# Raw left factors of the down projections in a queue of their own, loaded one use ahead of their split

## Chip, core and metric

The kernel runs on one core of a Trainium2 chip. The metric is the device time of one execution in microseconds (us). Before the change it is 1993.24 us, the median of three runs (1992.93 to 1993.47).

## The reference

One layer of a decoder trunk for 1024 prompt rows and 64 sample rows: an FFN (SwiGLU, 1024 to 2816 to 1024), a mixer (window attention and a gated linear recurrence side by side, between the projections `w_in` and `w_out`), and a second FFN, each between RMS norms and with a residual. All in float32. What the change concerns is the down projection of both FFNs:

```
def swiglu(x, w_gu, w_down):
    g, u = jnp.split(x @ w_gu, 2, axis=-1)
    return (jax.nn.silu(g) * u) @ w_down
```

## The kernel before

The 1088 rows stand in three blocks: block 0 (320 rows, the sample rows among them), and blocks 1 and 2 (384 rows each). A float32 product is made of three matmuls (`mm3`, L277 to L281): each operand is split into a rounded high part and a low rest. `split` (L257 to L259) does this with a cast on ScalarE (L258) and a subtraction on VectorE (L259).

Block 0's down projection is computed plainly (`down`, L906). Blocks 1 and 2 go together through a Strassen-like scheme of seven products, numbered 1 to 7. The up projection forms the left factors, seven for each pair of FFN columns, and stores them in DRAM as `FA` (L790, L792), and the right factors as `FB` and `FH`. The `pair` function (L995) reads them back: for each product m it runs over six groups of column pairs (`GROUPS`, five of two and one of one), and a group of two takes 18 matmuls, for three PSUM banks. `put` then adds a bank to the outputs on VectorE (L975), or for a product that starts an output copies it on ScalarE (L985 for product 5).

`begin_pair(ms, inner)` (L936) makes two queues for a list of products: `W`, the right factors, two ahead, and `AC`, the left factors, two ahead with inner=True and one ahead otherwise. A queue is an `Ahead` (L74): a list of functions, each of which issues a load and the split of its tile; `next` hands out the oldest tile and calls as many further functions as the depth asks for.

In a left factor's function, `act(m, ks)`, four things stand together: the tile `t` for the split halves, a raw tile (`ar` in the profile), its load from `FA` on SP's queue (L962), and the split. `t` is always one of eight slots named `h384` (`hslot(1)`, L67). The raw tile is one of four slots `wf` with inner=True; with inner=False it takes one of the same eight `h384` slots. These slots also hold `hmix[1]` and `hmix[2]`, the split inputs of `w_in` for blocks 1 and 2, four slots each (`new_h`, L302, called by `pre_n`, L444).

The first FFN runs its products as PA = (1, 6, 2) with inner=True, before the mixer; then (5, 3), (7,) and (4,) with inner=False, while the mixer of block 0 and the norms of blocks 1 and 2 run in between, in small portions at each `tick()`. The second FFN runs PA, (5, 3), (7,) and (4,), all with inner=True, at the kernel's end. The `last` argument of `down` and `pair` begins the next pair's queues before the last group of the current one.

Weights of products 1, 2, 3, 5 and 6 are loaded raw (L947, L950; three slots `raw`) and split into two of eight slots `wsp`; 7 and 4 of the first FFN are loaded as split halves (L941, L942).

SP issues nearly all loads, in order. The order of the instructions on each engine, and which slot a tile gets, are made by the kernel's scheduler from the program's order and a timeline of its own (`schedule_with_timeline_sim=True`, L1749); a tile may so be loaded long before the place where the program names it, if a slot is free.

Of the kernel before, what the change touches and what calls it, by code (L numbers as in the profile page):

```python
# [45 lines left out]
def tile_step(ctx: ExitStack, tc: tile.TileContext, A: dict, O: list):  # L46
# [10 lines left out]
    def uid(s):  # L57
        cnt[0] += 1
        return f"{s}_{cnt[0]}"
# [7 lines left out]
    def hslot(n):  # L67
        w = WIDTH[n]
        return pp.tile([P, 4, w], F32R, tag=f"h{w}", bufs=8 if w == 384 else 4, name=uid("h"))
# [20 lines left out]
    def rawslot(shape=(P, KC, P)):  # L90
        return pp.tile(list(shape), F32, tag="raw", bufs=NRAW, name=uid("raw"))
# [165 lines left out]
    def split(hi, lo, src, lo_eng=None):  # L257
        S.copy(hi, src)  # L258
        (lo_eng or V).tensor_tensor(lo, src, hi.bitcast(F32), op=ALU.subtract)  # L259
# [389 lines left out]
    def make_ffn(wgu, wdn, h, tag):  # L649
# [284 lines left out]
        GROUPS = [range(k, min(k + 2, NK)) for k in range(0, NK, 2)]  # L934

        def begin_pair(ms, inner):  # L936
            def weight(m, ks):
                n, k0 = len(ks), ks[0]
                if m in halves:
                    hi, lo = [pp.tile([P, 2, 512], F32R, tag="wsp", bufs=8, name=uid("w")) for _ in range(2)]  # L940
                    nc.sync.dma_start(hi[:, :n].bitcast(F32), FH[:, k0:k0 + n, halves[m]])  # L941
                    nc.sync.dma_start(lo[:, :n].bitcast(F32), FB[:, k0:k0 + n, {7: 0, 4: 2}[m]])  # L942
                    return hi, lo
                raw = rawslot((P, 2, 512))
                if m in (1, 2, 3):
                    r, half = (k0 if m == 1 else k0 + NK), m == 3
                    nc.sync.dma_start(raw[:, :n], wdn[r * P:(r + n) * P, half * 512:half * 512 + 512].rearrange(  # L947
                        "(k p) m -> p k m", p=P))
                else:
                    nc.sync.dma_start(raw[:, :n], FB[:, k0:k0 + n, {7: 0, 5: 1, 4: 2, 6: 3}[m]])  # L950
                hi, lo = [pp.tile([P, 2, 512], F32R, tag="wsp", bufs=8, name=uid("w")) for _ in range(2)]
                split(hi[:, :n], lo[:, :n], raw[:, :n])
                return hi, lo

            def act(m, ks):
                n, k0 = len(ks), ks[0]
                t = hslot(1).rearrange("p (k l) w -> p k l w", k=2)
                if inner:
                    raw = f.pool.tile([P, 2, 384], F32, tag="wf", bufs=4, name=uid("ar"))
                else:  # L960
                    raw = pp.tile([P, 2, 384], F32, tag="h384", bufs=8, name=uid("ar"))
                nc.sync.dma_start(raw[:, :n], FA[:, k0:k0 + n, SLOT[m]])  # L962
                split(t[:, :n, 1], t[:, :n, 0], raw[:, :n])
                return t

            W[ms] = Ahead([lambda m=m, ks=ks: weight(m, ks) for m in ms for ks in GROUPS])
            AC[ms] = Ahead([lambda m=m, ks=ks: act(m, ks) for m in ms for ks in GROUPS], 2 if inner else 1)
            W[ms].fill()
            AC[ms].fill()
# [595 lines left out]
    act, unit0, scaled = pre_first(xs[0], rows1, f1pre, h, [f1.raw0(c) for c in (first[0] * P, DFF + first[0] * P)], w0, part)  # L1565
# [187 lines left out]
```

## Time and profile before

| what | before |
|---|---|
| median of three runs | 1993.24 us |
| the profiled execution's own time | 1993.22 us |
| its span, first to last instruction | 1991.5 us |
| granted clock of TensorE, mean | 0.999 |
| loads `ar` from `FA` | 70 of 384 KB, 14 of 192 KB |
| data moved by DMA | 370.31 MB, 186 GB/s |
| FFN 1 pair PA, about | 576 to 646 us |
| FFN 1 pairs (5, 3), (7,), (4,), about | 728 to 846 us |
| FFN 2 pairs, about | 1822 to 1984 us |

A line of the profile gives an engine, the program's line (L258 is line 258), the operation, and the tiles as out<-in. PE is TensorE, PEld its weight loads, DVE VectorE, ACT ScalarE, POOL GpSimd; SPq is the queue of SP that issues loads. In a timeline the first two columns are start and duration in us, a bracket at the end is the idle time of the engine before the instruction and what ended it. In a list of waits stand the total in us, the number of times and the longest. Matmuls are pipelined, so one that is listed with 0.39 us can start 0.22 us after the one before it.

### The profile page before, as it was taken

To read this page: it belongs to the slowest core of one execution; us is meant where nothing else is said; L and a number is where in the kernel's file an instruction comes from. 1 tells how busy PE (TensorE), PEld (TensorE's weight loads), DVE (VectorE), ACT (ScalarE), POOL (GpSimd) and SP (SyncE) were. 2 spreads that over 40 slices of the span, in tenths; PEclk is the share of its full clock that TensorE was granted. 3 is DMA by queue.
4 is the path that set the end of the run, shared out by engine and by line. 5 is a ranking of instruction groups with operands and counts; after the bars stand their busy time and mean duration, and the time that the engine had idled before them with its cause. 6 is when DMAs were issued, how large, how long until landed. Compare 5 with 4: busy or idle time off the path is not lost.

```text
span 1991.5 us, 34618 instructions
## 1 busy us (share of the span) xinstructions
PE 1978.7 (99%) x13331; PEld 1854.6 (93%) x13331; DVE 1406.9 (71%) x2595; ACT 949.0 (48%) x1736; POOL 178.0 (9%) x244
## 2 busy tenths in 40 slices
PE   9999999999999999999999999999999999999998
PEld 8999999999998987797999898989999999999886
DVE  7686767886558656777667756756887877655667
ACT  5753334444445444445344444756544444444453
POOL 0000000000004101211113311220000000000201
PEclk9999999999999999999999999999999999999999
DMA  8735555755677647766434343527565555677874
GB/s 230 225 107 186 175 170 177 232 196 192 228 243 212 182 138 236 251 169 181 128 104 132 92 138 107 177 90 237 165 210 191 197 183 193 209 232 232 291 262 140
DMA packets 377319, 370.31 MB, mean 186 GB/s; under 512 B 40546, under 2 KB 294321, under 8 KB 377137
## 3 DMA queue, kind: packets, MB, share of 16 engines
q1 hardware_dynamic: 371169, 357.21, 56.9%
q10 hardware_dynamic: 5984, 10.88, 1.6%
q8 instruction: 105, 1.72, 0.4%
q14 instruction: 61, 0.50, 0.1%
HBM read 284.31 MB, written 84.71 MB: 185 GB/s over the span
## 4 chain that ended last, share of the span: by engine, by line
PE 96%; DMA 1%; DVE 1%; ACT 1%; issue 0%; SPq 0%; DVEq 0%; ACTq 0%
PE mm L279 28%; PE mm L280 28%; PE mm L281 28%; PE pv L1219 1%; PE c L281 1%; PE c L279 1%; PE c L280 1%; PE sc L1178 1%; PE pT L1206 1%; PE tr L511 1%; DMA ar<-fa 1%; PE lv L1251 1%; PE l L1274 0%; DMA raw<-in_ffn_w_gu_dram 0%; DMA xt<-in_x_prompt_dram 0%; PE av L1329 0%
## 5 line engine op out<-in xcount | busy, mean ns | idle before, releaser
L279 PE MATMUL mm<-h,wsph 128*128 128x320 f32 (+1 forms) x1280 | 407.3, 319 | 0.0
L280 PE MATMUL mm<-h,wsph 128*128 128x320 f32 (+1 forms) x1280 | 405.3, 317 | 0.0
L281 PE MATMUL mm<-h,wspl 128*128 128x320 f32 (+1 forms) x1280 | 403.6, 317 | 0.0
L258 ACT CAST wsph<-raw 128x1024 fp32r<-128x1024 f32 x200 | 209.1, 1048 | 269.6 <-PE mm L280 213.7
L259 DVE TENSOR_TENSOR wspl<-raw,wsph 128x1024 fp32r<-128x1024 f32 x200 | 247.7, 1240 | 125.3 <-ACT wsph L258 120.7
L258 ACT CAST w<-raw 128x512 fp32r<-128x512 f32 (+1 forms) x218 | 160.3, 740 | 209.2 <-PE mm L280 111.9
L259 DVE TENSOR_TENSOR w<-raw,w 128x512 fp32r<-128x512 f32 (+1 forms) x218 | 185.8, 856 | 87.6 <-ACT w L258 87.1
L279 PEld LDWEIGHTS mm<-h,wsph 128*128 128x128 f32 x1280 | 240.2, 188 | 3.8 <-issue 2.8
L281 PEld LDWEIGHTS mm<-h,wspl 128*128 128x128 f32 x1280 | 239.9, 188 | 2.8 <-issue 2.3
L280 PEld LDWEIGHTS mm<-h,wsph 128*128 128x128 f32 x1280 | 240.5, 188 | 1.5 <-issue 1.1
L279 PE MATMUL mm<-h,w 128*128 128x384 f32 (+1 forms) x720 | 240.3, 335 | 0.6 <-ACT w L258 0.5
L280 PE MATMUL mm<-h,w 128*128 128x384 f32 (+1 forms) x720 | 240.7, 335 | 0.0
L281 PE MATMUL mm<-h,w 128*128 128x384 f32 (+1 forms) x720 | 235.4, 334 | 0.0
L279 PE MATMUL mm<-w,h 128*128 128x512 f32 x462 | 181.1, 395 | 0.6 <-DVE big L975 0.6
L280 PE MATMUL mm<-w,h 128*128 128x512 f32 x462 | 181.3, 392 | 0.0
L281 PE MATMUL mm<-w,h 128*128 128x512 f32 x462 | 179.8, 391 | 0.0
L280 PE MATMUL mm<-big,w 128*128 128x384 f32 x528 | 176.5, 334 | 0.0
L279 PE MATMUL mm<-big,w 128*128 128x384 f32 x528 | 176.3, 334 | 0.0
L281 PE MATMUL mm<-big,w 128*128 128x384 f32 x528 | 176.2, 334 | 0.0
L279 PEld LDWEIGHTS mm<-h,w 128*128 128x128 f32 x720 | 135.0, 188 | 1.3 <-ACT w L258 0.7
L280 PEld LDWEIGHTS mm<-h,w 128*128 128x128 f32 x720 | 135.1, 188 | 0.1
L281 PEld LDWEIGHTS mm<-h,w 128*128 128x128 f32 x720 | 134.7, 188 | 0.1
(363 smaller groups left out, 3576.0 us busy)
## 6 DMA issues: line engine op xcount, KB each, us to landing
raw<-in_ffn_w_gu_dram SPq DMA_DIRECT2D x156, 512.0 KB
raw<-in_ffn_w_down_dram SPq DMA_DIRECT2D x74, 512.0 KB
raw<-in_w_in_dram SPq DMA_DIRECT2D x54, 512.0 KB
ar<-fa SPq DMA_DIRECT2D x70, 384.0 KB
big<-in_ffn_w_down_dram SPq DMA_DIRECT2D x88, 256.0 KB
fb<-big SPq DMA_DIRECT2D x44, 512.0 KB
fa<-big SPq DMA_DIRECT2D x22, 768.0 KB
raw<-fb SPq DMA_DIRECT2D x30, 512.0 KB
```

What stands on the lines that cost most here:

```text
L258: S.copy(hi, src)
L259: (lo_eng or V).tensor_tensor(lo, src, hi.bitcast(F32), op=ALU.subtract)
L279: PE.matmul(out, a[0], b[0], start=first, stop=False, skip_group_check=resume)
L280: PE.matmul(out, a[0], b[1], start=False, stop=False, skip_group_check=resume)
L281: return PE.matmul(out, a[1], b[0], start=False, stop=last, skip_group_check=resume).ins
L511: PE.transpose(bank[:, i * P:(i + 1) * P], y[kh][:, i, k * P:(k + 1) * P], ident)
L1178: PE.matmul(banks[g][:, i * 256:i * 256 + wk], zq[64 * g:64 * g + 64, 2 * pr + i, b * P:(b + 1) * P], kx[64 * g:64 * g + 64, k0:k0 + wk], ...
L1206: PE.transpose(bank[:, (i * nk + kb) * P:(i * nk + kb + 1) * P], pt[g][:, i, kb * P:(kb + 1) * P], ident)
L1219: PE.matmul(ob[:, hd * 64:hd * 64 + 64], pT[g][:, (i * nk + kb) * P:(i * nk + kb + 1) * P], vn[:, vb, g * 64:g * 64 + 64], start=kb == 0, ...
L1251: PE.matmul(b5[cs, n_, a], x[:, a, cs], y[:, a, cs], start=True, stop=True)
```

## The change

`act` loses its raw tile and its load to a new function `act_raw`; a second `Ahead` of depth 1, local to `begin_pair`, holds the raw tiles of all products and groups in the same order. `act` allocates `t` and then takes the next raw tile from this queue, and the queue issues the load of the following raw tile before `act` splits the one it took. The ring of slots is the same as before in either case. Loads, splits, their number and size are unchanged; `begin_pair` no longer issues as many loads as splits at its start, but one more.

```diff
-            def act(m, ks):
+            def act_raw(m, ks):
                 n, k0 = len(ks), ks[0]
-                t = hslot(1).rearrange("p (k l) w -> p k l w", k=2)
                 if inner:
                     raw = f.pool.tile([P, 2, 384], F32, tag="wf", bufs=4, name=uid("ar"))
                 else:
                     raw = pp.tile([P, 2, 384], F32, tag="h384", bufs=8, name=uid("ar"))
                 nc.sync.dma_start(raw[:, :n], FA[:, k0:k0 + n, SLOT[m]])
-                split(t[:, :n, 1], t[:, :n, 0], raw[:, :n])
+                return raw[:, :n]
+
+            raw = Ahead([lambda m=m, ks=ks: act_raw(m, ks) for m in ms for ks in GROUPS], 1)
+
+            def act(m, ks):
+                n = len(ks)
+                t = hslot(1).rearrange("p (k l) w -> p k l w", k=2)
+                split(t[:, :n, 1], t[:, :n, 0], raw.next())
                 return t
```

## Prediction

> **What bounds the kernel now.** I read the page first: busy time by engine, then the chain that ended last.
>
> ```profile
> PE 1978.7 (99%) x13331; PEld 1854.6 (93%) x13331; DVE 1406.9 (71%) x2595; ACT 949.0 (48%) x1736; POOL 178.0 (9%) x244
> PE 96%; DMA 1%; DVE 1%; ACT 1%; issue 0%; SPq 0%; DVEq 0%; ACTq 0%
> ```
>
> TensorE is busy for 1978.7 of 1991.5 us, and 96% of the chain is TensorE's own work. The change adds and removes no matmul, so it can gain only where TensorE stands still: 12.8 us in all. The second view, the waits of TensorE alone (us in total, times, longest), says where:
>
> ```profile
> PE ax L566 <- DVE sm L570: 1.1, 1, 1.1
> PE lv L1251 <- DVE big L1369: 1.1, 1, 1.1
> PE tr L598 <- DMA big<-in_x_sample_dram: 0.8, 1, 0.8
> PE mm L279 <- ACT wsph L258: 0.6, 1, 0.6
> PE mm L279 <- DVE big L975: 0.6, 2, 0.4
> PE mm L279 <- ACT w L258: 0.5, 1, 0.5
> PE spv L1405 <- DVE t L1400: 0.4, 1, 0.4
> ```
>
> They sum to 5.1 us; the rest is the stretch after the last matmul. Three (ax, tr and w) belong to the kernel's start, with the first rows of x. That leaves 1.1 + 0.6 + 0.6 + 0.4 = 2.7 us of waits in the whole body, whatever their cause. This is the bound on any gain by shorter waits.
>
> Third, what the tile `ar` (the raw left factor) makes others wait for, once as a row of all waits and once for 600 to 860 us alone:
>
> ```profile
> ACT h L258 <- DMA ar<-fa: 36.6, 16, 6.1
> ```
>
> ```profile
>   DMA ar<-fa: 36.6, 16
> ```
>
> ScalarE sits for 36.6 us on loads of `ar` from FA, all of it between 600 and 860 us. Those are the pairs of the first FFN called with inner=False (products 5, 3, 7, 4); the 36.6 us are the change's target. But ScalarE is 48% busy: its idle time counts only where TensorE waits behind it.
>
> The fourth view, windows, shows three stretches (the up projection, the inner=False pairs, a part of FFN 2's inner=True pairs); the columns are length, then busy us of PE, PEld, DVE, ACT, POOL:
>
> ```profile
> 25.00:478.00 453.00, 453.00 (x2782) 452.67 (x2781) 343.10 (x614) 214.86 (x404) 0.75 (x4) 1.00 0.57 184
> 728.00:846.00 118.00, 116.37 (x971) 93.12 (x970) 77.55 (x189) 52.98 (x126) 22.30 (x33) 1.00 0.71 225
> 1880.00:1920.00 40.00, 40.00 (x178) 33.10 (x178) 27.02 (x33) 21.62 (x32) 0.00 (x0) 1.00 0.78 253
> ```
>
> In FFN 2's pairs TensorE is idle for nothing at all; in the inner=False pairs for 118.00 − 116.37 = 1.63 us. That 1.63 us is what the target stretch has to give.
>
> **The change part by part.**
>
> *Inner pairs (PA of FFN 1, all pairs of FFN 2): nothing.* Their raw tiles are in the ring `wf` of four, and the loads already run ahead as far as that ring lets them. One load and the cast of its tile, from the first FFN and from the second:
>
> ```profile
> 516.57 0.93 SPq L962 DMA_DIRECT2D ar<-fa  x2
> ```
>
> ```profile
> 552.53 0.83 ACT L258 CAST h<-ar 128x768 fp32r<-128x768 f32 x1
> ```
>
> ```profile
> 1944.33 0.33 SPq L962 DMA_DIRECT2D ar<-fa  x1
> ```
>
> ```profile
> 1956.23 0.50 ACT L258 CAST h<-ar 128x384 fp32r<-128x384 f32 x1
> ```
>
> The first row holds PA's third and fourth loads, the second PA's fourth cast: 36 us later. In FFN 2 the last load is issued 11.9 us ahead of its cast. No cast waits for a load here (the 36.6 us lie elsewhere), so issuing one place earlier in the program changes no time. I cost it at 0; the cover is this lead, and without it TensorE would feel at most one load's flight per group.
>
> *The inner=False pairs: the load leaves the serial chain.* Their raw tile shares the eight slots `h384` with the split tiles, and there the loads go one by one, each just after the split before it:
>
> ```profile
> 734.83 0.37 SPq L962 DMA_DIRECT2D ar<-fa  x1
> ```
>
> ```profile
> 739.99 0.96 DVE L259 TENSOR_TENSOR h<-ar,h 128x768 fp32r<-128x768 f32 x1 [2.40 <-ACT h L258]
> ```
>
> ```profile
> 740.98 0.37 SPq L962 DMA_DIRECT2D ar<-fa  x1
> ```
>
> 739.99 + 0.96 = 740.95, and the next load is issued at 740.98: it waits for the slot that the split frees, so load, cast and split follow each other with a period of 6.15 us. A group's 18 matmuls take 4.1 us, at 40.00 / 178 = 0.225 us each (the window of FFN 2 above). This would starve TensorE, were it not for the split tiles made earlier:
>
> ```profile
> 627.30 0.84 ACT L258 CAST h<-ar 128x768 fp32r<-128x768 f32 x1 [2.14 <-DMA ar<-fa]
> ```
>
> ```profile
> 728.41 0.39 PE L279 MATMUL mm<-w,h 128*128 128x512 f32 x1
> ```
>
> Product 5's first cast is at 627.30; its matmuls run around 728. So ScalarE's waits of up to 6.1 us mostly eat a stock of finished tiles. They reach TensorE in one place, where VectorE stands in order behind such a split:
>
> ```profile
> 753.90 0.34 SPq L962 DMA_DIRECT2D ar<-fa  x1
> ```
>
> ```profile
> 756.34 0.51 ACT L258 CAST h<-ar 128x384 fp32r<-128x384 f32 x1 [2.51 <-DMA ar<-fa]
> ```
>
> ```profile
> 753.87 1.23 DVE L259 TENSOR_TENSOR w<-raw,w 128x1024 fp32r<-128x1024 f32 x1
> 756.89 0.56 DVE L259 TENSOR_TENSOR h<-ar,h 128x384 fp32r<-128x384 f32 x1 [1.79 <-ACT h L258]
> 757.36 0.29 DVE L1269 COPY_PREDICATED cm<-lm,lv 128x128 f32<-128x128 uint8 x1
> 757.99 1.28 DVE L975 TENSOR_TENSOR big<-mm,big 128x512 f32<-128x512 f32 x2
> ```
>
> ```profile
> 758.12 0.46 PE L1251 MATMUL lv<-t,t 128*32 128x32 f32 x32 [1.06 <-DVE big L1369]
> 758.74 0.50 PE L279 MATMUL mm<-w,h 128*128 128x512 f32 x1 [0.15 <-DVE big L975]
> ```
>
> VectorE is free at 755.10 (753.87 + 1.23), waits 1.79 us for the cast, which waited 2.51 us for the load; behind the split stand L1269, the copy at L1369 and the additions of `put` (L975), and for the last two TensorE waits 1.06 + 0.15 = 1.21 us. With the raw tile landed, VectorE starts 1.79 us sooner and all 1.21 us go. Late next is nothing that I see: L1269 starts as the split ends, so it only queued. The price lies between 0 (another wait ends there instead) and 1.21 us; I take 1.21, as the rows show one queue and one cause.
>
> The other 0.42 us of the 1.63 stay:
>
> ```profile
> 817.14 0.75 DVE L439 SCALAR_TENSOR_TENSOR big<-big,sm,xt 128x512 f32<-128x512 f32 x1 [3.97 <-DMA xt<-in_x_prompt_dram]
> ```
>
> ```profile
> 822.37 0.50 PE L279 MATMUL mm<-w,h 128*128 128x512 f32 x1 [0.42 <-DVE big L975]
> ```
>
> There VectorE was late by a load of `xt`, which the change doesn't touch.
>
> *The load that moves, and SP's queue.* The number of loads and their bytes stay. Each `ar` load is passed one weight load ahead (L947, L950, or the two of L941 and L942), and at the start of each of eight pairs one more `ar` goes ahead of the third weight. One issue takes 0.34 to 0.37 us on SP, and a flight of half a tile (the short last group) at most 756.34 − 753.90 = 2.4 us, so a whole one less than 4.9 us. The cover is the weights' lead:
>
> ```profile
> 706.37 0.37 SPq L950 DMA_DIRECT2D raw<-fb  x1
> ```
>
> That is product 5's first weight, 22 us before 728.41. Without the cover a start would cost up to one flight. I take 0.
>
> *The wait that is added.* A load now sits one place earlier on SP and may wait there for a slot; behind it on SP stand weights and the `xt` loads. SP's own waits at that line before:
>
> ```profile
> SPq L962 <- DVE h L259: 27.4, 44, 1.8
> ```
>
> 0.6 us each, at most 1.8 us. A wait of this size is lost in 22 us of lead: 0.
>
> *One more live tile among eight.* Two raws instead of one can be live, so one finished split tile fewer. The stock shrinks by one group, 4.1 us; product 5's first tile was 101 us old when it was used. Taken as 0. The other end is the place where the slots change hands, at the end of product 4:
>
> ```profile
> 839.67 1.05 ACT L472 ACTIVATE h<-tr,cols 128x384 fp32r<-128x384 f32 x2
> ```
>
> ```profile
> 840.26 1.97 SPq L962 DMA_DIRECT2D ar<-fa  x1
> ```
>
> ```profile
> 845.03 0.51 ACT L258 CAST h<-ar 128x384 fp32r<-128x384 f32 x1 [3.81 <-DMA ar<-fa]
> ```
>
> `pre_n`'s `new_h(1)` takes four of the eight slots from 839.67 on, just when the last `ar` wants one. From issue to cast it needed 845.03 − 840.26 = 4.8 us.
>
> *Sum*, against the profiled execution's 1993.22 us (span 1991.5 and 1.7 around it; the median of the runs shown is 1993.24): 1993.2 − 1.2 = 1992.0 us.
>
> **The rivals.**
>
> *Nothing arrives sooner.* If the extra raw only gets its slot when the split frees one, the chain stays serial, or TensorE's 1.2 us turn up behind another in-order wait. For: at 740.98 the slot ended the wait, not the place in the program. Against: by then the stock is being used up, so slots come free. 1993.2 us.
>
> *Slower: the new raw holds a slot that `new_h(1)` wants.* It decides if the last raws and `pre_n` overlap around 840 us: `hmix[1]` is then late by the 4.8 us above, and w_in of block 1, which needs all its columns, has TensorE standing. 1993.2 + 4.8 = 1998.0 us. For: eight slots, four of them taken there at once. Against: the last `ar` could also be gone earlier, and TensorE has mixer work beside it. The Trainium skill, Trace Analysis, section Optimization Strategy, speaks for this side: a gap that repeats on the engine that should be full can mean that buffer space for the next tile is lacking. By that rule the cure is more slots, not earlier loads; TensorE's waits here are single ones, so the trace has no repeating gap.
>
> *Much faster: TensorE is not as full as it looks.* In the pairs PEld is busy for 33.10 of 40.00 us, in the up projection for 452.67 of 453.00. Were the missing 17% a wait for operands, as large in all pairs (2 FFNs × 7 products × 3 banks × 11 × 3 = 1386 matmuls × 0.225 = 312 us), 0.17 × 312 = 53 us would be hidden and some of it could come back: 1940 us at the far end. Against: the spacing is as regular where tiles are long finished:
>
> ```profile
> 1979.55 0.39 PE L281 MATMUL mm<-w,h 128*128 128x512 f32 x1
> 1979.77 0.39 PE L279 MATMUL mm<-w,h 128*128 128x512 f32 x1
> ```
>
> 0.22 us here, over 20 us after the last cast (1956.23); a matmul of 512 columns simply takes longer than its weight load. The Trainium skill, Trace Analysis, section Identifying the Most-Contended Engine, holds matmul busy time a bad measure and takes the busy share of LDWEIGHTS instead; by that rule this rival would have room, and the even spacing speaks against it.
>
> **How the numbers follow.** Forecast 1992.0: 0.62. Nothing arrives sooner, 1993.2: 0.20. Slower by the slots, 1998.0: 0.13. Much faster: 0.05. About 0.2% (4.0 us) is what a measurement of this kernel can tell from no change: faster means below 1989.2, slower above 1997.2. The first two cases lie within, so same 0.82, slower 0.13, faster 0.05. The range: below, all 2.7 us of waits in the body gone, 1993.2 − 2.7 = 1990.5; above, the slot case, 1998.0.
>
> **What would show it.** Right: ScalarE's wait for `ar` falls from 36.6 us towards 10 or less; TensorE's 1.06 and 0.15 us near 758 are gone; loads of `ar` in the inner=False pairs are issued before the split ahead of them ends; FFN 2's windows stay at 40.00 of 40.00. Wrong: TensorE waits of microseconds in 728 to 900, above all for `h` of w_in after product 4; `ar` loads still issued in step with the splits. The order on the engines is made by the kernel's scheduler, so a new order with new single waits elsewhere, each of the size seen (0.4 to 1.1 us), would also spoil the sum.

## The result, and the profile after

| what | before | after |
|---|---|---|
| median, 20 executions each | 1993.09 us | 1997.13 us |
| lowest to highest | 1990.73 to 1995.93 | 1993.69 to 1999.76 |
| the profiled execution's own time | 1993.22 us | 1997.48 us |
| its span | 1991.5 us | 1995.8 us |
| granted clock of TensorE, mean | 0.999 | 0.998 |

After over before is 1.0021 (95% interval 1.0015 to 1.0027): 4.0 us slower, where the forecast was 1992.0 us and faster. That is at the bound that the prediction set for "slower": just beyond its 0.2%, and just under its figure of 1997.2 us.

Busy time by engine and the shares of the chain of the kernel after:

```profile
PE 1983.1 (99%) x13331; PEld 1858.5 (93%) x13331; DVE 1409.6 (71%) x2595; ACT 949.8 (48%) x1736; POOL 177.5 (9%) x244
PE 96%; DMA 2%; DVE 1%; ACT 1%; issue 0%; SPq 0%; DVEq 0%; ACTq 0%
```

The same 13331 matmuls, but TensorE is busy for 4.4 us more. The change's target is gone all the same; the wait of ScalarE for `ar` from FA was 36.6 us before:

```profile
ACT h L258 <- DMA ar<-fa: 0.3, 1, 0.3
```

The windows of two stretches show the gain and the loss side by side (columns as in the prediction; the third number from the end is TensorE's granted clock), first before, then after:

```profile
750.00:775.00 25.00, 23.79 (x196) 18.87 (x195) 14.15 (x33) 11.47 (x25) 3.78 (x8) 1.00 0.63 180
825.00:850.00 25.00, 25.00 (x184) 20.94 (x183) 19.43 (x44) 13.86 (x28) 5.55 (x8) 1.00 0.62 175
```

```profile
750.00:775.00 25.00, 25.00 (x203) 20.03 (x202) 14.15 (x32) 12.30 (x26) 4.88 (x8) 1.00 0.69 204
825.00:850.00 25.00, 22.22 (x153) 18.20 (x152) 16.86 (x41) 12.85 (x27) 3.77 (x7) 0.86 0.49 138
```

From 750 to 775 us TensorE gains 25.00 − 23.79 = 1.21 us, the forecast gain to the hundredth. From 825 to 850 us it stands still for 25.00 − 22.22 = 2.78 us, where it had not stood at all, and its clock drops to a mean of 0.86. FFN 2's pairs are full, as before:

```profile
1884.00:1924.00 40.00, 40.00 (x179) 33.10 (x178) 27.01 (x32) 21.87 (x32) 0.00 (x0) 1.00 0.77 256
```

The waits of TensorE name the two new places. The 1.06 us at 757 us and the wait at 822 us are no longer in the list; these stand at its head:

```profile
PE pv L1225 <- ACT t L1215: 1.4, 1, 1.4
PE lv L1257 <- DVE sm L252: 1.2, 1, 1.2
```

Lines behind the edit have moved by 6: L1215 is the copy of pT that was L1209, L1275 and L1291 were L1269 and L1285. The place is in the mixer of block 0: pT are transposed attention weights, pv their product with the values, lv a level of the gated recurrence; beside them run the streams of the norms, `pre_n(1)` and `half_n`. The timelines of TensorE, VectorE and ScalarE there, after:

```profile
825.85 0.39 PE L280 MATMUL mm<-w,h 128*128 128x512 f32 x1
827.46 0.46 PE L1257 MATMUL lv<-t,t 128*32 128x32 f32 x32 [1.22 <-DVE sm L252]
828.04 1.10 PE L1225 MATMUL pv<-vn,t 128*128 128x64 f32 x8
830.58 1.97 PE L1225 MATMUL pv<-vn,t 128*128 128x64 f32 x8 [1.44 <-ACT t L1215]
...
832.88 0.63 PE L279 MATMUL mm<-w,h 128*128 128x512 f32 x1
833.31 0.63 PE L280 MATMUL mm<-w,h 128*128 128x512 f32 x1
```

```profile
822.72 1.66 DVE L439 SCALAR_TENSOR_TENSOR big<-big,sm,xt 128x512 f32<-128x512 f32 x1
825.23 0.16 DVE L400 SCALAR_TENSOR_TENSOR sm<-sm 128x3 f32<-128x3 f32 x1 [0.85 <-ACT junk L394]
...
826.61 0.16 DVE L251 SCALAR_TENSOR_TENSOR sm<-sm 128x3 f32<-128x3 f32 x1
826.69 0.29 DVE L1275 COPY_PREDICATED cm<-lm,lv 128x128 f32<-128x128 uint8 x1
826.89 0.42 DVE L1291 TENSOR_TENSOR t<-t,t 128x256 f32<-128x256 f32 x1
```

```profile
828.74 1.32 ACT L458 ACTIVATE big<-big,sm 128x512 f32<-128x512 f32 x2
829.97 0.56 ACT L1215 COPY t<-pT 128x512 f32<-128x512 f32 x1
```

VectorE first waits 0.85 us for a sum of squares, then runs `pre_n(1)`'s root chain (L400 and `rsqrt`), and only then the two small steps of the mixer for which TensorE stands (lv starts 0.15 us after L1291 ends; the list puts the wait down to L252, which runs beside it). ScalarE makes its half of the copy of pT only after `half_n`'s squares and two scalings (L458); pv's second half starts as that copy ends, 829.97 + 0.56. Before, VectorE had these steps the other way round:

```profile
823.57 0.30 DVE L1269 COPY_PREDICATED cm<-lm,lv 128x128 f32<-128x128 uint8 x1
823.76 0.72 DVE L1285 TENSOR_TENSOR t<-t,t 128x256 f32<-128x256 f32 x1
...
825.46 0.68 DVE L1209 COPY t<-pT 128x512 f32<-128x512 f32 x1
826.39 0.32 DVE L400 SCALAR_TENSOR_TENSOR sm<-sm 128x3 f32<-128x3 f32 x1 [0.25 <-ACT junk L394]
```

ScalarE's copy of pT stood ahead of `half_n`'s squares, the first of which (L415) ran at 826.95:

```profile
823.77 0.57 ACT L1209 COPY t<-pT 128x512 f32<-128x512 f32 x1
```

Behind the second wait matmuls of 512 columns start 0.43 us apart (832.88, 833.31) in place of 0.227. The windows show why; the clock is the third number from the end:

```profile
826.00:828.00 2.00, 0.70 (x34) 0.38 (x32) 1.87 (x9) 1.43 (x4) 0.00 (x0) 1.00 1.00 335
828.00:830.00 2.00, 1.10 (x8) 0.97 (x8) 1.26 (x3) 1.91 (x6) 0.77 (x1) 0.76 0.80 301
830.00:832.00 2.00, 1.42 (x7) 1.42 (x7) 0.90 (x3) 1.25 (x3) 1.24 (x4) 0.50 0.24 90
832.00:834.00 2.00, 2.00 (x7) 1.71 (x7) 1.71 (x4) 0.00 (x0) 0.03 (x1) 0.50 0.00 0
834.00:836.00 2.00, 2.00 (x6) 1.52 (x6) 1.22 (x3) 0.69 (x2) 0.00 (x0) 0.54 0.00 0
836.00:838.00 2.00, 2.00 (x24) 1.43 (x23) 0.86 (x4) 1.49 (x4) 0.79 (x1) 1.00 0.00 0
```

The mean of 0.76 from 828 to 830 us is a fall to 0.50 at about 829.0 us, just ahead of the second wait (829.14 to 830.58). Of the loss, 2.78 us are waits; the slow clock costs the busy part of each slow window times what is missing of the clock: 1.42 × 0.50 + 2.00 × 0.50 + 2.00 × 0.46 = 2.6 us. Together 5.4 us in this stretch. Less the 1.2 us gained at 757 us and the 0.4 us of the wait at 822 us that is 3.8 of the 4.3 us by which the span grew; the rest is spread over the stretch from 850 to 1350 us, with gains and losses in it.

### The profile page after: what moved, and what is told of

It is laid out like the page before. It is cut to its first block, busy times and chain, and to the rows that moved or that the text cites. A ratio compares the mean times of both kernels' runs of the same rounds, so it can differ in the third digit from the quotient of the medians.

```text
span 1995.8 us, 34621 instructions
## 1 busy us (share of the span) xinstructions
PE 1983.1 (99%) x13331; PEld 1858.5 (93%) x13331; DVE 1409.6 (71%) x2595; ACT 949.8 (48%) x1736; POOL 177.5 (9%) x244
## 4 chain that ended last, share of the span: by engine, by line
PE 96%; DMA 2%; DVE 1%; ACT 1%; issue 0%; SPq 0%; DVEq 0%; ACTq 0%
PE mm L279 28%; PE mm L281 28%; PE mm L280 28%; PE pv L1225 1%; PE c L279 1%; PE c L281 1%; PE c L280 1%; PE sc L1184 1%; PE pT L1212 1%; PE lv L1257 1%; PE tr L511 1%; PE l L1280 0%; DMA xt<-in_x_prompt_dram 0%; DMA raw<-in_ffn_w_gu_dram 0%; DMA w<-fb 0%; PE av L1335 0%
```

## Experiments

**Theory O** (order): the loads cost nothing; the scheduler gave VectorE and ScalarE another order near 825 us, and that order makes TensorE wait. **Rival L** (loads): loading earlier, or the extra tile in the eight slots, costs by itself. **Rival N**: every new order loses at some place, whatever brought it about. **Theory C** and **theory S** are about the clock and stand at e8 and e15.

All that follow compute the whole reference; e8 and e15 add a tail of matmuls behind its last output, so that their time isn't compared, and e13 and e14 are one execution each. In the table, "over before" is against the median of the kernel before on the same chip; the next columns are of one trace each: TensorE's busy time from 750 to 775 and from 825 to 850 us (of 25.00), and the granted clock in the latter.

| kernel | median us | over before us | ratio (95% interval) | 750 to 775 | 825 to 850 | clock |
|---|---|---|---|---|---|---|
| before | | | | 23.79 | 25.00 | 1.00 |
| after | 1997.13 | +4.0 | 1.0021 (1.0015 to 1.0027) | 25.00 | 22.22 | 0.86 |
| e1 only inner=True pairs | 1992.45 | +0.1 | 1.0000 (0.9991 to 1.0008) | 23.68 | 25.00 | 1.00 |
| e2 after, both orders put back | 1992.55 | +0.2 | 1.0001 (0.9992 to 1.0010) | 25.00 | 24.19 | 1.00 |
| e3 before, same orders written down | 1992.29 | −0.1 | 1.0001 (0.9992 to 1.0010) | 23.77 | 25.00 | 1.00 |
| e4 before, part of after's order | 1995.59 | +3.2 | 1.0016 (1.0007 to 1.0025) | 23.81 | 24.24 | 1.00 |
| e5 only product 4 | 1997.91 | +6.1 | 1.0026 (1.0018 to 1.0035) | 23.98 | 23.38 | 0.93 |
| e6 all but product 4 | 1996.39 | +4.5 | 1.0021 (1.0012 to 1.0030) | 25.00 | 22.73 | 0.93 |
| e7 after, VectorE's order put back | 1995.08 | +3.2 | 1.0014 (1.0005 to 1.0023) | 25.00 | 22.73 | 1.00 |
| e9 before, rate 0.7 | 2000.70 | +8.2 | 1.0039 (1.0027 to 1.0052) | 23.80 | 22.39 | 1.00 |
| e10 after, rate 0.7 | 1999.47 | +6.9 | 1.0033 (1.0020 to 1.0045) | 25.00 | 21.58 | 0.97 |
| e11 before, rate 0.8 | 1998.12 | +5.6 | 1.0028 (1.0017 to 1.0040) | 23.89 | 22.30 | 1.00 |
| e12 after, rate 0.8 | 1998.97 | +6.4 | 1.0031 (1.0019 to 1.0042) | 25.00 | 23.01 | 0.93 |

**e1, only the inner=True pairs.** `early` is `inner`:

```diff
+            early = inner
...
-                split(t[:, :n, 1], t[:, :n, 0], raw.next())
+                split(t[:, :n, 1], t[:, :n, 0], raw.next() if early else act_raw(m, ks))
```

> Only the pairs with inner=True load one use ahead; the inner=False pairs (products 5, 3, 7, 4 of the first FFN) load as before. The order of the work on VectorE, ScalarE and SP stays that of the kernel before. Theory O (the time was lost to a new order of VectorE and ScalarE near 825 us, which the loads of the inner=False pairs set off): within 0.5 us of the kernel before, ScalarE's wait for ar still about 36 us. Rival L (earlier loads themselves cost, by SP, the rings or the DMA queues): some of the 4 us shows here too, 1 to 3 us over before, because FFN 2 has most of the pairs with inner=True.

Measured: 1992.45 us, as before; ScalarE waits 35.5 us for `ar` between 600 and 860 us. The pairs with inner=True have nothing to do with the loss, and the prediction's 0 for them holds.

**e2, the changed kernel with two orders put back.** VectorE's root chain is placed behind the copy of pT, ScalarE's squares of `half_n` behind its copy of pT; `behind(i, pred)` orders instruction i behind pred on its engine, without a semaphore, and the squares are issued behind `PIN["act"]`:

```diff
...
-                    (S.copy if g else V.tensor_copy)(t[:, :2 * wk], bank[:, :2 * wk])
+                    cp_ = (S.copy if g else V.tensor_copy)(t[:, :2 * wk], bank[:, :2 * wk])
+                    if "stt" in PIN and g == 0:
+                        behind(PIN.pop("stt"), cp_.ins)
+                        PIN["two"] = 1
+                    elif "two" in PIN and g == 1:
+                        PIN.pop("two")
+                        PIN["act"] = cp_.ins
...
```

> The changed kernel with all its loads one use ahead, but two orders near 825 us put back as the kernel before has them: pre_n(1)'s root chain on VectorE behind the copy of pT, and half_n's squares on ScalarE behind ScalarE's copy of pT. Theory O: the 5.5 us lost between 825 and 850 us go, no TensorE wait over 0.5 us there, granted clock 1.00 in every window; about 1 to 2 us below before, 1991 to 1992.5 us. Rival L (the loads, or the extra tile in the eight slots): it stays at about 1997 us. Rival N (any new order costs some us somewhere): 1993 to 1997 us, with new waits at another place.

Measured: 1992.55 us, 0.2 us over before. The loads are all one use ahead (ScalarE waits 0.3 us for `ar`, TensorE has 25.00 of 25.00 from 750 to 775 us), and the 4 us are gone. L is out: the loss hangs on the order. How little of the order that is can be read from the traces. In the sequence of all instructions TensorE's is the same, and on VectorE and ScalarE e2 differs from the changed kernel by four alone: VectorE's copy_predicated, the step behind it and the copy of pT stand ahead of the root chain, and ScalarE's copy of pT ahead of the squares. From the kernel before, e2 still differs in dozens of places from 627 us on, and costs nothing; so N doesn't hold of every new order. But the 1.2 us do not show in the median; in the trace a new wait stands near the old place:

```profile
PE oT L1170 <- DVE t L1166: 0.8, 1, 0.8
```

**e3, the control**: the same lines in the kernel before.

> Control: the kernel before with the same two orders written down that it has anyway. All theories: within 0.5 us of the kernel before; a difference beyond that would be the price of writing the order down, to be taken off the run of the changed kernel with it.

Measured: 1992.29 us, 0.1 us under before: writing the order down costs nothing. In e1 and e3 the sequences on VectorE and ScalarE are those of before, instruction by instruction.

**e4, before's loads with a part of after's order.** The root chain goes ahead of L1269 and of the copy of pT, ScalarE's copy behind the second scaling:

```diff
+        if n == 1:
+            behind(PIN["cp"], PIN["rs"])
+            PIN["v"] = PIN["rs"]
...
+                    if "v" in PIN and g == 0:
+                        behind(cp_.ins, PIN.pop("v"))
```

> The kernel before with its own loads, but near 825 us the order that the changed kernel has: pre_n(1)'s root chain on VectorE ahead of attention's copy_predicated and copy of pT, and ScalarE's copy of pT behind half_n's squares and the two scalings. Theory O: slower by 3 to 5.5 us (1996 to 1998.5 us), TensorE waits of 1 to 1.5 us each for the copy of pT and for copy_predicated near 826 to 831 us, and a granted clock of about 0.5 in some windows behind them. Rival L: within 0.5 us of before, for no load is moved. If the waits come and the clock stays at 1.00: 2 to 3.5 us, and the clock was an accident of the changed kernel.

Measured: 1995.59 us, 3.2 us slower, within the range of O. Yet the trace doesn't bear out how. The scheduler, told of the order, moved TensorE's work too: 37 matmuls between the transposes pT and lv, where the changed kernel has 18 and the kernel before 21. And the step that lv waits for in the changed kernel (L1291 there, L1302 in e4) wasn't tied: it ran at 822.62, ahead of the root chain. So e4 isn't the changed kernel's order at that step. TensorE waits 0.8 us in 825 to 850 us and the clock is 1.00. The trace is of the quickest of the 11 executions (1993.75 us).

**e5, only product 4 one use ahead**: `early` is `not inner and ms == (4,)`.

> Only the last inner=False pair (product 4) loads one use ahead, all else as before. In this program VectorE has pre_n(1)'s root chain ahead of the copy of pT, TensorE has 18 matmuls between the transposes pT and the next lv, as in the changed kernel. Theory O: slower by 3 to 5.5 us, the two TensorE waits near 826 to 831 us and the low clock behind them are there, and the wait of 1.1 us at 757 us stays (so 1995.5 to 1998 us). Rival L (the loads themselves, spread over the three pairs): about a third of the 4 us, 1993.5 to 1994.5 us. Rival N: no forecast of its own.

Measured: 1997.91 us, 6.1 us slower. One pair of three does all of the harm; L wanted a third of it. VectorE has the order of the changed kernel at this place, TensorE waits for lv and for pv (0.83 and 0.68 us), and the clock falls to a mean of 0.93.

**e6, all pairs but that one**: `early` is `inner or ms != (4,)`.

> Every pair but the last inner=False one (product 4) loads one use ahead. In this program VectorE has the copy of pT ahead of pre_n(1)'s root chain, as in the kernel before. Theory O: no loss near 826 us, the wait at 757 us gone: 0 to 1.5 us below before. Rival L: two thirds of the loss, 1994.5 to 1996 us.

Measured: 1996.39 us, 4.5 us slower: theory O in its narrow form has fallen. The order that it names is the good one here, and the loss comes by another step of the same norm streams. VectorE and TensorE in e6:

```profile
831.43 0.43 DVE L408 TENSOR_SCALAR gb<-gb 128x512 f32<-128x512 f32 x1 [2.19 <-DMA gb<-in_norm_ffn_post_dram]
831.97 1.90 DVE L420 TENSOR_TENSOR big<-big,gb 128x512 f32<-128x512 f32 x3
833.78 0.29 DVE L1276 COPY_PREDICATED cm<-lm,lv 128x128 f32<-128x128 uint8 x1
```

```profile
834.54 0.56 PE L1281 MATMUL l<-t,t 128*32 128x32 f32 x16 [1.85 <-DVE t L1292]
```

`half_n`'s gain row waits 2.19 us for its load, its three multiplications take 1.90 us, and behind them stand the mixer's copy_predicated (L1269 of before) and the step that TensorE waits for. In the kernel before, copy_predicated comes between the first and the other two multiplications, at 830.64. Rival N gains: here another new order puts another norm step ahead of a mixer step.

**e7, only VectorE's order put back** in the changed kernel: e2 without `PIN["act"]`.

> The changed kernel with only VectorE's order near 825 us put back (pre_n(1)'s root chain behind the copy of pT); ScalarE's copy of pT stays behind half_n's squares. Theory O: the first TensorE wait (1.2 us for lv) goes, the second (1.4 us for ScalarE's copy of pT) stays at 1 to 2 us; with a single wait the granted clock stays 1.00, so 1 to 2 us over the run with both orders put back, about 1994 us. If the clock falls all the same: 1996 us. Rival L: 1997 us.

Measured: 1995.08 us, 3.2 us over before, some 3 us over e2. The wait for lv is gone, ScalarE's late copy still holds pv for 1.02 us, a new wait of 1.14 us (oT) stands at 841.68, and the clock stays at 1.00. So each of the two orders has its own price: e7 and e2 have the same sequence on VectorE, and on ScalarE they differ by the copy of pT alone, which stands behind the squares in e7. The size was expected as 1 to 2 us.

**e9 to e12, other schedules with and without the change.** The rate of the norm streams is all that differs, 0.7 or 0.8:

```diff
-    RA0, RA1, RB0, RB1 = 1.2, 0.75, 0.6, 0.8
+    RA0, RA1, RB0, RB1 = 1.2, 0.7, 0.6, 0.8
```

> The kernel before, with the rate of the norm streams RA1 at 0.7 in place of 0.75, as one more schedule. VectorE has the copy of pT ahead of pre_n(1)'s root chain. All theories: a schedule of its own, within 2 us of before; it is the base of the next kernel.

> The changed kernel with RA1 = 0.7. VectorE has the copy of pT ahead of the root chain, TensorE 21 matmuls between the transposes pT and lv, as in the kernel before. Theory O: none of the 4 us; 1.5 us faster to 0.5 us slower than the kernel before with RA1 = 0.7. Rival L: 4 us slower than it.

> The kernel before with RA1 = 0.8. VectorE has the copy of pT ahead of the root chain. All theories: within 2 us of before; the base of the next kernel.

> The changed kernel with RA1 = 0.8. VectorE has the root chain ahead of the copy of pT and TensorE 18 matmuls between the transposes pT and lv, as in the changed kernel at 0.75. Theory O: slower than the kernel before with RA1 = 0.8 by 2 to 5.5 us, with the two TensorE waits of 1 us and more near 826 to 831 us. Rival L: 4 us slower here and at 0.7 alike. If it is no slower, the order on VectorE is not enough for the loss.

Measured: all four are 5.6 to 8.2 us over before; the expectation of 2 us for the two bases was far off. With before's own loads, e9 and e11 lose 2.6 and 2.7 us of TensorE's time in the very stretch from 825 to 850 us. In e9, 1.97 + 0.18 us of that are waits for another load, of the sample rows' cache (`kv`), and e10 waits 2.56 + 0.38 us for it:

```profile
847.85 0.63 PE L1367 MATMUL skT<-ident,kv 128*128 128x128 f32 x4 [1.97 <-DMA kv<-in_cache_k_win_dram]
```

One of e11's three waits there (1.00, 0.70 and 0.94 us) is that of e6:

```profile
831.37 1.89 DVE L420 TENSOR_TENSOR big<-big,gb 128x512 f32<-128x512 f32 x3
833.18 0.29 DVE L1269 COPY_PREDICATED cm<-lm,lv 128x128 f32<-128x128 uint8 x1
```

```profile
833.94 0.56 PE L1274 MATMUL l<-t,t 128*32 128x32 f32 x16 [1.00 <-DVE t L1285]
```

No load of `ar` has been moved in either: losses of this size in this stretch come without the change too, and not only by norm steps. At the same rate the change is worth 1999.47 − 2000.70 = −1.2 us at 0.7, +0.9 us at 0.8 and +4.0 us at 0.75; with the order held (e2 and e3) +0.3 us. The differences at 0.7 and 0.8 are within the intervals. So e10 and e12 speak for a weaker N: what the change does to the time is the difference of two orders, and most orders seen here are slower than that of 0.75 without the change; e2's is as good. Whether 0.75 was once chosen because its order is good isn't on record.

**e8, the clock by itself.** Behind the last output of the kernel before stand bursts of 60 matmuls of 512 columns with waits of TensorE between them:

```diff
...
+        for stalls in [p for _ in range(8) for p in ((0,), (0, 0), (1, 1), (6,))]:
+            bank = burst(60, rhs)
+            for j, e in enumerate(stalls):
+                rhs = stall(bank, e)
+                if j < len(stalls) - 1:
+                    bank = burst(7, rhs)
...
```

> The kernel before, and behind its last output 33 bursts of 60 matmuls of 512 columns (the gains of the kernel are left as they are; only this tail is added, some 500 us, so the time isn't compared). Between the bursts TensorE is made to wait for VectorE, in turn, eight times each: once for about 1 us; twice for about 1 us with 7 matmuls between; twice for about 1.5 us with 7 matmuls between; once for about 4 us. Theory C (the halved clock of the changed kernel follows from the share of idle time in a stretch of some 4 to 5 us): 1.00 after single waits of 1 us, 0.5 in some or all of the double waits of 1.5 us and of the waits of 4 us, and matmuls 0.43 us apart in these places. Rival (only one unbroken idle time of over 3 us does it): 0.5 only behind the waits of 4 us.

Measured: the waits came out shorter than meant (0.78, 1.11 and 2.75 us). No burst behind a single or double wait has a matmul at the low clock, up to the pairs of waits shown by the first two rows; behind the long wait of the third row it is eight of eight, 7 or 8 matmuls at 0.43 us each:

```profile
2039.35 1.88 PE L1708 MATMUL mm<-pw,pw 128*128 128x512 f32 x7 [1.11 <-DVE pw L1715]
2042.34 13.90 PE L1708 MATMUL mm<-pw,pw 128*128 128x512 f32 x60 [1.11 <-DVE pw L1715]
2059.00 7.35 PE L1708 MATMUL mm<-pw,pw 128*128 128x512 f32 x24 [2.75 <-DVE pw L1715]
```

So waits of 1.11 us between full bursts don't do it, and those of the changed kernel, 1.22 and 1.44 us, were not much longer. What differs there is the work between the waits: 32 matmuls of 32 columns and 8 of 64. Which stretch theory C would have to count over, e15 shows.

**e13, e14: second looks** at e4 and at the changed kernel, without an edit.

> The kernel before with the new order near 825 us once more, for a trace of another execution: the first one was of the quickest execution (1993.75 us, where the median is 1995.59 us) and held no loss near 825 us. Theory O2 (a new order leaves waits of about 1 us next to groups of small matmuls, and the clock falls behind them in some executions): a time of 1995 to 1997 us, and 1.5 to 3 us more than in the first trace in one or two places with a granted clock under 1. Rival (the 3.2 us are spread): no place with more than 0.5 us.

> The changed kernel once more, for a trace of another execution. Theory O2: the two waits near 826 to 831 us are there again with 1.2 and 1.4 us within 0.3 us, since the order is the same; the clock falls behind them again, for 2 to 7 us. If the clock stays at 1.00 here, its 1.9 us belong to some executions only, and the kernel's time should then be about 1995 us.

e13: 1993.88 us where one execution of before had 1991.19 us on that chip. TensorE is busy for 23.82 of 25.00 us from 825 to 850 us, with one wait of 1.2 us (at 846.57, for `h`), and the clock is 1.00 everywhere. That is 1.2 us; the rest of e4's 3.2 us is not found in either trace and stays open.

e14: 1995.70 us. The two waits are there again, the second one shorter:

```profile
828.10 0.46 PE L1257 MATMUL lv<-t,t 128*32 128x32 f32 x32 [1.27 <-DVE sm L252]
830.49 1.10 PE L1225 MATMUL pv<-vn,t 128*128 128x64 f32 x8 [0.70 <-ACT t L1215]
```

Here the clock stays at 1.00 and the stretch loses 25.00 − 22.91 = 2.1 us in place of 5.4. So the waits belong to the changed kernel's order, and the low clock to some of its executions. The low clock isn't all of the loss: e14's span, 1994.0 us, is still 2.5 us over that of before's trace; 2.1 − 1.2 = 0.9 us of that lie in the two stretches of the table, and the rest is open. The 20 executions of the result agree on the whole: the three with a mean clock of 0.999 took 1993.69, 1995.12 and 1995.92 us, the three with 0.997 took 1998.37, 1998.42 and 1998.89 us, and the fourteen with 0.998 lie between 1995.48 and 1999.76 us.

**e15, small matmuls and the clock.** A second tail behind the kernel before, with groups of 32 float32 matmuls of 32 columns ("s") between waits (digits) and bursts:

```diff
...
+            for p in ("2", "4", "1s", "1s1", "s1s1", "s1sb1"):
...
```

> The second probe behind the kernel before (only this tail is added, so the time isn't compared): bursts of 60 matmuls of 512 columns, and between them in turn, six times each: one wait of about 1.6 us; one of about 2.3 us; a wait of 1.3 us and 32 matmuls of 32 columns; these and a wait of 1.3 us more; 32 small ones ahead of that as well; 32 small, a wait, 32 small, 4 large, a wait. Theory S (matmuls of 32 columns count as idle time for the clock): 1.00 behind waits of 1.6 us and behind one wait with small matmuls, 0.5 behind two waits of 1.3 us with small matmuls between, whose sum is about 3 us. Rival (only waits count, unbroken): 1.00 behind all of them, and 0.5 at most behind the wait of 2.3 us.

Measured: the groups came out far longer than meant (8.5 to 13.8 us, each matmul two rows of the trace, against 0.46 us in the kernel). That makes the answer plainer. Windows of a burst and, from 2274.70 us, a small group, with no wait between them:

```profile
2274.00:2276.00 2.00, 2.00 (x17) 1.86 (x15) 0.00 (x0) 0.00 (x0) 0.00 (x0) 1.00 0.00 0
2276.00:2278.00 2.00, 2.00 (x21) 2.00 (x20) 0.00 (x0) 0.00 (x0) 0.00 (x0) 1.00 0.00 0
2278.00:2280.00 2.00, 2.00 (x21) 2.00 (x20) 0.00 (x0) 0.00 (x0) 0.00 (x0) 1.00 0.00 0
2280.00:2282.00 2.00, 2.00 (x14) 2.00 (x13) 0.00 (x0) 0.00 (x0) 0.00 (x0) 0.60 0.00 0
```

TensorE is busy for 2.00 of 2.00 us all along, and some 6 us into the group the clock is halved. For the clock, these small matmuls count as little or nothing. Single waits of 1.8 us between bursts had slow matmuls behind them five times in five, one of 1.59 us none; waits of about 2.5 us five times in six. Theory S holds in that point; what a group of only 0.46 us does was not tried by itself.

The wait of about 2.5 us that did nothing shows what is counted. The traces' record of the clock changes on a grid of 3.41 us: all low stretches that end before the span does are 3.41 us long or a whole multiple of it (6.83 us in after). A stretch of that grid with the wait of 2.46 us, the one with a wait of 1.80 us, and the one behind the latter:

```profile
2024.39:2027.80 3.41, 1.70 (x7) 1.42 (x8) 1.48 (x6) 0.00 (x0) 0.00 (x0) 1.00 0.00 0
2181.43:2184.84 3.41, 1.61 (x8) 1.02 (x7) 1.61 (x6) 0.00 (x0) 0.00 (x0) 1.00 0.00 0
2184.84:2188.25 3.41, 3.41 (x10) 2.64 (x9) 0.00 (x0) 0.00 (x0) 0.00 (x0) 0.50 0.00 0
```

The longer wait (2023.64 to 2026.10) lies across two stretches, with at most 1.71 us idle in one; the shorter lies in one and leaves it idle for 1.80 us. All single waits between full bursts in e8 and e15 go this way: behind a stretch idle for 1.80 us or more the clock is halved (18 of 18), behind 1.71 us or less it is not. The repeats of one wait stand at nearly the same place of the grid, so these are few independent cases.

## Why the prediction was wrong, point by point

- **The bound and the removed wait: right.** ScalarE's 36.6 us fell to 0.3, TensorE's 1.21 us from 750 to 775 us went, in every traced kernel whose loads there are early (after, e2, e6, e7, e10, e12, e14: 25.00 of 25.00) and in none of the others. The wait of 0.42 us at 822 us, said to stay, went too in the trace of after.
- **Inner pairs at 0: right** (e1; FFN 2's window).
- **SP's queue, the moved load, the added wait at 0: right.** SP's wait for `h` at the load is 30.0 us in 47 times after, 0.6 us each, as before; nothing behind it became late.
- **The extra tile in eight slots at 0: right.** After has no TensorE wait for `h` of w_in. The rival that it carried, 1998.0 us, was near the measured time by chance: it put the loss at 840 us, by slots; it lies at 826 to 836 us, by order.
- **"Late next is nothing that I see": this step failed.** It asked what was late next in the order of before, and the order did not stay. The prediction named the scheduler only among what would spoil the sum, with "new single waits elsewhere, each of the size seen (0.4 to 1.1 us)". There were two, 1.2 and 1.4 us, side by side, and in that execution the clock was halved there, which cost 2.6 us more. So the term put at nothing, what comes late next, was 5.4 us in the stretch from 825 to 850 us. e2 showed that the order is what counts (four instructions put back take away the 4 us), e9 and e11 that losses of 2.6 and 2.7 us stand in that stretch with before's loads as well.
- **The chances.** Having counted a new order as a mishap at the end, the text gave no case to it. Ten programs here have an order on VectorE and ScalarE that differs from before's (after, e2, e4 to e7, e9 to e12); nine are slower than before, by 3.2 to 8.2 us, and e2 is as fast.

How the scheduler came to another order is only argued: it plans with a timeline of its own, in which a split that no longer waits leaves VectorE free earlier, for whichever step is then ready. What can be shown is that product 4's loads alone turn it (e5), the other pairs' loads turn it in another way (e6), and a rate of 0.7 or 0.8 in yet another (e9, e11). Open are the part of e4's 3.2 us that no trace holds, the part of e14's time outside the two stretches, and why the scheduler's own order at 0.75 without the change is better near 825 us than its others.

## What to carry to other kernels

Where a scheduler makes the order of the engines, an edit can be two edits: what it says, and a new order; here, with few waits left, the second was the larger, 5.4 us lost against 1.2 us gained in the profiled execution. Before pricing a removed wait, look for the stretch where small steps of one stream stand beside long steps of another on an in-order engine, and ask what a swap there would cost. To measure an edit for itself, hold the old order in place at that stretch and run the kernel before with the same lines as a control.

## What the hardware showed

TensorE's clock fell while TensorE was busy. In e15 it was halved some 6 us into a run of 32-column matmuls, with 2.00 of 2.00 us busy in each window. At the low clock 512 columns take 0.43 us in place of 0.227, for 3.41 us (e5, e6, e12) or 6.83 us (after).

Where a wait falls on the grid of 3.41 us matters as much as how long it is: in e15 a wait of 2.46 us across two stretches left the clock at 1.00, and one of 1.80 us within one halved it. The changed kernel fits this, though no run tested it there. Its clock fell at 829.02 us, at the end of a stretch (825.61 to 829.02) with 0.63 us of 512-column matmuls, a wait of 1.22 us and otherwise matmuls of 32 and 64 columns; the second wait, of 1.44 us, came after that, in the next stretch, and the stretch behind it was at the low clock too. In e14, counted back from its low clock at 1989.31 us, the stretch began at 825.40, with 1.43 us of 512-column matmuls ahead of the first wait, and the clock stayed.

The Trainium skill, TensorE: Matmul & The Clock Gate, section What's actually happening (in Part 1), gives half the clock after an idle window of about 3.4 us, a window that runs freely, so that the same kernel varies between executions. The grid of 3.41 us and the variation between after and e14, which differ in nothing else, agree with that. A whole window of idle time wasn't needed here: 1.80 us of 3.41 halved the clock in e15, and in the changed kernel 1.34 us of idle time did, with small matmuls beside it.
